# The first block of x in a slot of its own, 64 bytes out of step with the other fifteen

## The chip, the cores and the metric

The kernel runs on one core of one Trainium2 chip. The metric is the device time of one execution in microseconds, as the median of several runs. A profile of one execution stands beside the runs.

## The reference, cut to what matters

A decoder trunk of two layers on x of 256 tokens by 2048 features: an RWKV-7 time mix, a gated feed-forward layer with a causal convolution, a gated DeltaNet, and a second feed-forward layer, each followed by a layer norm of `ALPHA * x + f(x)`. Nearly all of the arithmetic is the product of x, or of a mixture of x with its shifted self, with large weight matrices:

```
r = xr @ w_r ; k = xk @ w_k ; v = xv @ w_v         # 2048 x 2048 each
proj = x @ w_in                                    # DeltaNet: 2048 x 12352
h = causal_dwconv(x @ w_up, conv_w) + conv_b       # feed-forward, twice: 2048 x 11008
gate, up = jnp.split(h, 2, axis=-1)
return (jax.nn.silu(gate) * up) @ w_down
```

## The kernel before, in words

**Blocks of x.** The 2048 features of an x are 16 blocks of 128. A block is one tile of 128 partitions by 512 float32r values: 256 tokens of the high part, then 256 of the low part (`split_act`, L677, makes the two: a rounded copy, and the rest). A product of two numbers so split takes three matmuls: high by high, high by low, low by high.

**Projections.** `proj_fm` (L687) makes up to 256 output features of a projection. Four times it loads 512 rows of weights into a tile `raw`, which ScalarE rounds into `whi` and VectorE (or GpSimd) turns into `wlo` (`weights`). Per block k of x and half b of the output there are three matmuls, with 128 columns of `whi` or `wlo` as the stationary operand and 256 columns of the block as the moving one; in the profile they are `mm<-xhl,whi` and `mm<-xhl,wlo`, or `mm<-mixhl,..` in the RWKV stage. They go k = 0 to 15 in order, 96 to a projection of 256 outputs, and every block is read again by every projection. For k = 0 the order of the three is high, high, low; for all others low, high, high:

```
for kk in range(4):
    for b in range(nb):
        for lo in (False, True) if i + kk == 0 else (True, False):
            product(tiles[i], i, kk, b, lo, ts)
```

The k projections (8) read an x that lies in slots of the RWKV stage's own pool (`slot`, L1063). The v projections (8) and r projections (8) read blocks that `mix` (L1066) takes from the pool `keep`. The up-projections of a feed-forward layer (`ffn`, L1507) are 22 for the gate and 22 for the up half, the last of each half as wide; DeltaNet (`gdn`, L1538) has 48 and a narrow one for its gates. Their x (`xhl`) is made by `ln_part` (L867): blocks 0 to 7 in `keep`, 8 to 15 in a pool of the stage (`hp`).

**The pool `keep`** has one kind of slot, `hl`, 2048 bytes per partition, 16 of them (`kept`, L670). At first they hold the 16 blocks of xv and then of xr; from the output projection of the RWKV stage on, 8 of them hold the residual `res` (L1211) to the end, and 8 the first half of x. In DeltaNet's output projection, the even ones of the 32 blocks `ohl` (L1640) take slots of `keep` too, the odd ones those of the stage. The last part of that projection keeps the blocks of seven weight tiles, 14 blocks, until the second half of the tokens is done.

**Addresses.** In the program as allocated, all weight tiles (`whi`, `wlo`, 4096 bytes each) begin at 0 modulo 128 bytes within a partition, every slice of them that a matmul loads too, and all blocks of x, in whichever pool, at 64 modulo 128. The tiles of a DeltaNet unit (`KQhi`, `KQlo`, both operands of the matmuls `kk`, and `S0hi`, `S0lo`) begin at 96.

**What sets the order.** A planner writes out the order of every engine's instructions beforehand (`Plan.order`): it goes by estimated costs, by which buffers of a pool are free, and fills TensorE's waits in the RWKV and DeltaNet units with projection matmuls. The up-projections have no such units beside them: there TensorE runs projection matmuls alone. SyncE issues all loads of weights.

The functions that the diff touches, and what calls them:

Of the kernel before, what the change touches and what calls it, by code (L numbers as in the profile page):

```python
# [13 lines left out]
F32R = mybir.dt.float32r  # L14
# [5 lines left out]
P = 128  # L20
T = 256
D = 2048
KB = D // P
# [596 lines left out]
class Trunk:  # L620
# [48 lines left out]

    def kept(self, dt, name):  # L670

        return self.keep.tile([P, 512], dt, tag="hl", bufs=KB, name=name)

    def hl(self, name, kept=False):
        return self.kept(F32R, name) if kept else self.hp.tile([P, 512], F32R, tag="hl", bufs=self.nhl, name=name)
# [191 lines left out]
    def ln_part(self, tb, chs):  # L867

        nc = self.nc
        gname, bname, li = self.ln  # L870
        for ch in chs:
            self.ln_norm(tb, ch)
            ps = self.sd("lnT")
            for j in range(4):
                kb = ch * 4 + j
                if tb == 0:
                    self.xk.append(self.hl("xhl", kb < KB // 2))
                self.tr(ps[:, j * P:(j + 1) * P], self.res[tb][ch][:, j * P:(j + 1) * P])
            for j in range(4):
                kb = ch * 4 + j  # L880
                t = self.tp.tile([P, P], F32, tag="lnt", bufs=NLNT, name="lnt")
                x, g, b = ps[:, j * P:(j + 1) * P], self.par(gname, li * KB + kb), self.par(bname, li * KB + kb)
                nc.either(("vector", "tensor_scalar", (t, x, g, b, ALU.mult, ALU.add), {}),
                          ("scalar", "activation", (t, x, AF.Identity), dict(scale=g, bias=b)))
                hi, lo = (self.xk[kb][:, o + tb * P:o + (tb + 1) * P] for o in (0, T))
                nc.copy(hi, t)
                nc.two(lo, t, hi.bitcast(F32), ALU.subtract)
# [178 lines left out]
    def mix(self, m, xk, ks=range(KB)):  # L1066

        for k in ks:
            x = self.slot([P, 512], F32R) if m == 2 else self.kept(F32R, "mixhl")
            t = self.xp.tile([P, T], F32, tag="mixt", bufs=3, name="mixt")  # L1070
            self.mixed(m, k, t)
            self.split_act(x[:, :T], x[:, T:], t)
            xk.append(x)
# [816 lines left out]
```

## Time and profile before

| | us |
|---|---|
| median of 3 runs (lowest, highest) | 3112.8 (3108.89, 3115.27) |
| the profiled execution | 3106.09 |
| its span, first to last instruction | 3104.4 |
| TensorE busy | 2996.5 (97% of the span) |
| its weight loads busy | 2801.8 (90%) |
| VectorE busy | 2163.8 (70%) |
| ScalarE busy | 1584.3 (51%) |
| GpSimd busy | 669.8 (22%) |

In order of time, the span holds the k, v and r projections with the RWKV units and the output projection (to about 695 us), the first feed-forward layer (up to 1190, down to 1430 us), DeltaNet (to about 2165 us) and its output projection (to 2370 us), and the second feed-forward layer. A busy TensorE isn't TensorE at its best: matmuls overlap in the records (one of 256 columns is recorded with 276 to 281 ns, though the next begins after some 113 to 118 ns), so how fast they follow each other is read by counting them in a stretch, or from their start times.

### The profile page before, as it was taken

What the parts mean: (1) busy time and instruction counts of PE and PEld (TensorE: products, weight loads), DVE (VectorE), ACT (ScalarE), POOL (GpSimd) and SP (SyncE); (2) the same over time, 40 slices, a digit from 0 to 9 for tenths busy, and PEclk for the clock granted to TensorE, in tenths of its full rate; (3) what the DMA queues carried; (4) which work ended last, traced back from release to release, by engine and by line L of the source; (5) the groups of instructions that cost most, each with busy time, mean ns of one, the idle gap of its engine ahead of it and who ended that gap; (6) DMA issues with size and microseconds to landing.
All of it is one profiled execution on the core that took longest, in us unless ns stands there. A gap on an engine that the chain in (4) does not pass through costs nothing.

```text
span 3104.4 us, 56128 instructions
## 1 busy us (share of the span) xinstructions
PE 2996.5 (97%) x22371; PEld 2801.8 (90%) x22371; DVE 2163.8 (70%) x3421; ACT 1584.3 (51%) x2584; POOL 669.8 (22%) x576
## 2 busy tenths in 40 slices
PE   8999999999999999998999999999999999999998
PEld 7998898779999998887999999998788999999886
DVE  7657878867666665447888888888677666666445
ACT  4436666445555554335455555555466555555333
POOL 3014334425101010003221121113143410101001
PEclk9998999999999999999999999999999999999999
DMA  6652222236666665655555555554455666666655
GB/s 198 207 165 87 67 65 89 71 119 202 189 186 188 185 188 183 194 192 161 171 148 146 144 148 147 153 144 129 149 189 181 203 185 189 184 189 185 192 190 186
DMA packets 436262, 503.77 MB, mean 162 GB/s; under 512 B 22784, under 2 KB 367264, under 8 KB 436000
## 3 DMA queue, kind: packets, MB, share of 16 engines
q1 hardware_dynamic: 436000, 500.19, 53.8%
q8 instruction: 175, 2.87, 0.4%
q14 instruction: 87, 0.71, 0.1%
HBM read 498.00 MB, written 2.13 MB: 161 GB/s over the span
## 4 chain that ended last, share of the span: by engine, by line
PE 82%; DVE 10%; POOL 3%; issue 2%; ACT 2%; DMA 1%; SPq 0%; DVEq 0%; POOLq 0%; ACTq 0%
PE mm L558 51%; PE tm L558 22%; DVE wlo L558 3%; PE y L558 1%; ACT whi L558 1%; PE au L558 1%; DVE uc L558 1%; PE n L558 1%; PE gm L558 1%; PE kv L558 1%; POOL lt L558 1%; POOL xhl L558 0%; PE o L558 0%; PE yT L558 0%; PE u L558 0%
## 5 line engine op out<-in xcount | busy, mean ns | idle before, releaser
L558 DVE TENSOR_TENSOR wlo<-raw,whi 128x1024 fp32r<-128x1024 f32 (+1 forms) x898 | 1113.5, 1241 | 629.6 <-ACT whi L558 626.9
L558 PE MATMUL mm<-xhl,whi 128*128 128x256 f32 x8584 | 1532.3, 283 | 5.1 <-DVE xhl L558 2.7
L558 ACT CAST whi<-raw 128x1024 fp32r<-128x1024 f32 (+2 forms) x917 | 939.5, 1026 | 854.4 <-PE mm L558 508.0
L558 PEld LDWEIGHTS mm<-xhl,whi 128*128 128x128 f32 x8584 | 1318.8, 190 | 8.2 <-POOL xhl L558 3.3
L558 PE MATMUL mm<-xhl,wlo 128*128 128x256 f32 (+1 forms) x4376 | 1212.1, 282 | 3.9 <-DVE wlo L558 3.1
L558 PEld LDWEIGHTS mm<-xhl,wlo 128*128 128x128 f32 x4376 | 819.4, 189 | 5.1 <-DVE wlo L558 3.4
L558 PE MATMUL tm<-whi,hhl 128*128 128x512 f32 x1312 | 406.6, 390 | 0.0
L558 DVE SCALAR_TENSOR_TENSOR acc<-mm,taps,acc 128x255 f32<-128x255 f32 (+1 forms) x522 | 248.3, 479 | 77.1 <-ACT acc L558 69.4
L558 PEld LDWEIGHTS tm<-whi,hhl 128*128 128x128 f32 x1312 | 246.3, 188 | 56.2
L558 PE MATMUL mm<-mixhl,whi 128*128 128x256 f32 x1536 | 281.6, 285 | 12.7 <-ACT mixhl L558 8.2
L558 POOL TENSOR_TENSOR hhl<-acc,hhl 128x256 fp32r<-128x256 f32 x84 | 101.4, 1208 | 755.9 <-ACT hhl L558 755.9
L558 PE MATMUL tm<-wlo,hhl 128*128 128x512 f32 x656 | 258.5, 394 | 0.8 <-DVE wlo L558 0.8
L558 PEld LDWEIGHTS mm<-mixhl,whi 128*128 128x128 f32 x1536 | 240.8, 195 | 16.1 <-ACT mixhl L558 8.2
L558 PE MATMUL mm<-mixhl,wlo 128*128 128x256 f32 x768 | 221.3, 293 | 4.7 <-DVE wlo L558 3.8
L558 ACT ACTIVATE acc<-mm,taps 128x256 f32<-128x256 f32 x230 | 124.1, 540 | 150.5 <-PE mm L558 150.3
L558 PE MATMUL tm<-whi,ohl 128*128 128x512 f32 x480 | 156.7, 399 | 0.1
L558 PEld LDWEIGHTS mm<-mixhl,wlo 128*128 128x128 f32 x768 | 147.4, 194 | 8.6 <-DVE wlo L558 4.8
L558 PEld LDWEIGHTS tm<-wlo,hhl 128*128 128x128 f32 x656 | 123.3, 188 | 25.6 <-DVE wlo L558 1.1
L558 POOL TENSOR_TENSOR wlo<-raw,whi 128x1024 fp32r<-128x1024 f32 (+2 forms) x19 | 44.0, 2315 | 444.9 <-ACT whi L558 440.8
L558 PEld LDWEIGHTS tm<-whi,ohl 128*128 128x128 f32 x480 | 90.7, 189 | 19.7 <-DVE z_u L558 0.7
L558 PE MATMUL tm<-wlo,ohl 128*128 128x512 f32 x240 | 94.0, 392 | 1.3 <-DVE wlo L558 1.3
L558 PE MATMUL tm<-whi,yhl 128*128 128x512 f32 x224 | 86.8, 427 | 1.4 <-ACT r_u L558 0.8
(342 smaller groups left out, 3349.6 us busy)
## 6 DMA issues: line engine op xcount, KB each, us to landing
raw<-in_ffn_w_up SPq DMA_DIRECT2D x336, 512.0 KB, 3.8
raw<-in_gdn_w_in SPq DMA_DIRECT2D x192, 512.0 KB, 3.8
raw<-in_ffn_w_down SPq DMA_DIRECT2D x168, 512.0 KB, 4.2
raw<-in_gdn_w_out SPq DMA_DIRECT2D x64, 512.0 KB, 3.8
raw<-in_rw_w_v SPq DMA_DIRECT2D x32, 512.0 KB, 4.3
raw<-in_rw_w_r SPq DMA_DIRECT2D x32, 512.0 KB, 3.6
raw<-in_rw_w_o SPq DMA_DIRECT2D x32, 512.0 KB, 3.7
raw<-in_rw_w_k SPq DMA_DIRECT2D x31, 512.0 KB, 4.5
```

Source lines behind the costliest of these rows:

```text
L558: i = getattr(getattr(self.real, o.eng), fn)(*(val(a) for a in args), **{k: val(a) for k, a in kw.items()})
```

## The change

Block 0 of every x that lies in `keep` gets a slot of its own, `x0`, of 544 values (2176 bytes per partition), and lies 16 values, 64 bytes, behind its beginning. The slots of the other kind become 15 instead of 16. `mix` and `ln_part` take block 0 there and the other blocks from the 15. `res` and `ohl` have only the 15 to choose from. The k projections' x and blocks 8 to 15 of `xhl` stay as they are. 2176 bytes are a multiple of 128, so that whatever lies behind keeps its place modulo 128; block 0 then begins at 0 modulo 128, where all the others begin at 64.

```
     def kept(self, dt, name):
 
-        return self.keep.tile([P, 512], dt, tag="hl", bufs=KB, name=name)
+        return self.keep.tile([P, 512], dt, tag="hl", bufs=KB - 1, name=name)
+
+    def block(self, k, name):
+
+        return self.kept(F32R, name) if k else self.keep.tile([P, 544], F32R, tag="x0", name=name)[:, 16:528]
...
                 if tb == 0:
-                    self.xk.append(self.hl("xhl", kb < KB // 2))
+                    self.xk.append(self.block(kb, "xhl") if kb < KB // 2 else self.hl("xhl"))
...
         for k in ks:
-            x = self.slot([P, 512], F32R) if m == 2 else self.kept(F32R, "mixhl")
+            x = self.slot([P, 512], F32R) if m == 2 else self.block(k, "mixhl")
```

## Rows read from the trace of the kernel before

**Rows 1.** The page, busy time of TensorE, and its granted clock in 40 slices.

```profile
PE 2996.5 (97%) x22371; PEld 2801.8 (90%) x22371; DVE 2163.8 (70%) x3421; ACT 1584.3 (51%) x2584; POOL 669.8 (22%) x576
...
PEclk9998999999999999999999999999999999999999
```

**Rows 2.** The page, the chain that ended last, by engine and by line.

```profile
PE 82%; DVE 10%; POOL 3%; issue 2%; ACT 2%; DMA 1%; SPq 0%; DVEq 0%; POOLq 0%; ACTq 0%
PE mm L558 51%; PE tm L558 22%; DVE wlo L558 3%; PE y L558 1%; ACT whi L558 1%; PE au L558 1%; DVE uc L558 1%; PE n L558 1%; PE gm L558 1%; PE kv L558 1%; POOL lt L558 1%; POOL xhl L558 0%; PE o L558 0%; PE yT L558 0%; PE u L558 0%
```

**Rows 3.** Stretches: busy us and instructions by engine, granted clock, DMA share, GB/s.

```profile
60.00:160.00 100.00, 100.00 (x884) 100.00 (x884) 63.02 (x87) 43.67 (x51) 2.94 (x2) 1.00 0.65 202
...
800.00:900.00 100.00, 100.00 (x851) 100.00 (x851) 62.25 (x80) 51.98 (x72) 9.72 (x8) 1.00 0.64 186
2500.00:2600.00 100.00, 100.00 (x851) 100.00 (x850) 62.08 (x80) 51.97 (x71) 10.93 (x9) 1.00 0.64 185
```

**Rows 4.** Groups by form, TensorE, in 60 to 160 and in 800 to 900 us.

```profile
L558 PE MATMUL mm<-mixhl,whi 128*128 128x256 f32 x590 | 99.8, 276 | 0.0
...
L558 PE MATMUL mm<-xhl,whi 128*128 128x256 f32 x568 | 99.7, 281 | 0.0
```

**Rows 5.** Timeline of TensorE (start, duration), in the v projection.

```profile
177.01 0.33 PE L558 MATMUL mm<-mixhl,wlo 128*128 128x256 f32 x1
177.18 0.40 PE L558 MATMUL mm<-mixhl,whi 128*128 128x256 f32 x2
```

**Rows 6.** Groups by form, TensorE, 178 to 196 us.

```profile
L558 PE MATMUL mm<-mixhl,whi 128*128 128x256 f32 x103 | 18.2, 281 | 0.0
L558 PE MATMUL mm<-mixhl,wlo 128*128 128x256 f32 x52 | 14.4, 281 | 0.0
```

**Rows 7.** Timeline of TensorE in the DeltaNet stage, behind `au` and behind `du`.

```profile
1656.82 0.83 PE L558 MATMUL au<-u,lt 128*128 128x128 f32 x6
...
1658.98 0.39 PE L558 MATMUL mm<-xhl,whi 128*128 128x256 f32 x2
...
1659.55 0.56 PE L558 MATMUL du<-rhr,y 128*128 128x128 f32 x4
...
1660.47 0.40 PE L558 MATMUL mm<-xhl,whi 128*128 128x256 f32 x2
```

**Rows 8.** Timeline: from the first and the last resumed stretch of that stage.

```profile
1512.68 0.39 PE L558 MATMUL mm<-xhl,whi 128*128 128x256 f32 x2
...
2158.16 0.39 PE L558 MATMUL mm<-xhl,whi 128*128 128x256 f32 x2
```

**Rows 9.** Timeline: `kk` without a wait: its first, and the next projection matmul.

```profile
1526.67 0.28 PE L558 MATMUL kk<-KQhi 128*128 128x256 f32 x1
...
1527.39 0.40 PE L558 MATMUL mm<-xhl,whi 128*128 128x256 f32 x2
...
1980.84 0.28 PE L558 MATMUL kk<-KQhi 128*128 128x256 f32 x1
...
1981.55 0.28 PE L558 MATMUL mm<-xhl,wlo 128*128 128x256 f32 x1
```

**Rows 10.** Stretches: both up-projections (TensorE alone); DeltaNet's output projection, all engines.

```profile
720.00:1180.00 460.00, 460.00 (x3909) 1.00 0.65 188
2380.00:2850.00 470.00, 470.00 (x3989) 1.00 0.65 188
...
2165.00:2370.00 205.00, 200.44 (x992) 164.74 (x991) 149.02 (x233) 113.12 (x197) 61.22 (x54) 0.99 0.52 169
```

**Rows 11.** Groups by form, TensorE, DeltaNet stage, 1440 to 2160 us.

```profile
L558 PE MATMUL mm<-xhl,whi 128*128 128x256 f32 x3020 | 542.3, 283 | 1.3 <-DVE xhl L558 1.3
L558 PE MATMUL mm<-xhl,wlo 128*128 128x256 f32 x1507 | 427.8, 288 | 0.0
```

**Rows 12.** Timeline: a `kk` that began after a wait, and the fast pace behind.

```profile
1612.25 0.28 PE L558 MATMUL kk<-KQhi 128*128 128x256 f32 x1
...
1613.72 0.39 PE L558 MATMUL mm<-xhl,whi 128*128 128x256 f32 x2
```

## The prediction

> **What bounds the kernel now.** I first read the page's busy shares: TensorE is busy for 97% of the span, with the granted clock at nine tenths or more in 39 of 40 slices and at eight in the other [rows 1]. The chain of waits agrees: 82% of the time to the last instruction lies on TensorE, 51% in the projections `mm`, whose moving operand is a block of x [rows 2]. So what matters is how fast consecutive projection matmuls follow each other, and that is read by counting them. In 100 us of the first projection (w_k) the engine starts 884 of them, one per 113.1 ns; in 100 us of either feed-forward up-projection it starts 851, one per 117.5 ns [rows 3]. Clock (1.00), shape and busy share (100.00 of 100 us) are the same, and the instruction itself lasts 276 ns in the one and 281 ns in the other [rows 3, 4]. There are thus two paces, **fast** and **slow**, 4.4 ns apart, with no idle time in either.
>
> The pace sticks. In the v projection a single late matmul (0.17 us to the next instead of 0.11) at 177.01 us ends the fast pace, and the 155 matmuls of the stretch 178 to 196 us all last 281 ns [rows 5, 6]. The up-projections run without a break and are slow from end to end. In the DeltaNet stage, where other small matmuls keep breaking in, the pace is drawn anew at each resumption: after `au` the projection runs fast, after `du`, 2.5 us later in the same projection, slow (where the timeline merges two matmuls, the pair takes 0.39 us at the fast pace and 0.40 us at the slow) [rows 7]. Over that stage I followed every resumption of 16 or more projection matmuls behind another tile: 66 stretches, 39 of them fast and 27 slow after the first few (the first and the last, both fast, are shown) [rows 8]. By count of matmuls the stage is about half and half.
>
> So the pace is not fixed by where x and the weights lie: the same addresses run at both. It is a phase between the matmul's stream and the weight load that runs beside it all the time (TensorE and its loader are both busy for 100.00 of 100 us [rows 3]). What starts a new phase can end the slow pace.
>
> **The change part by part.** *Block 0 moves by 64 bytes modulo 128.* In the program before, weight tiles begin at 0 and all blocks of x at 64 modulo 128; block 0 would now begin at 0, like the weights. It is read by the first 6 matmuls of each projection's 96, in 8 v, 8 r, 88 up and 49 DeltaNet projections, 153 in all (a few are narrower and have 3); the k projections keep their own slots. Nearest to such a matmul are the six `kk` matmuls of a DeltaNet unit: 256 columns too, in the same order of high and low parts, with both operands at 96 modulo 128. Their six take 0.72 us from 1526.67 us and 0.71 us from 1980.84 us, 118 to 120 ns each [rows 9]. Directly, block 0 costs between -4.4 and +2.5 ns a matmul against the slow pace: x 6 x 153 = -4.0 to +2.3 us. I take +1 us, near `kk`.
>
> *What the six do to the pace behind them* is the term that counts. No row shows this very disturbance, so I bound it. At best every slow stretch turns fast. The two uninterrupted up-projection stretches hold 3909 and 3989 matmuls in 460 and 470 us [rows 10]; at 113.1 ns the 7898 would take 893 us, 37 us less. The DeltaNet stage has 3020 + 1507 projection matmuls [rows 11], half slow: 2264 x 4.4 ns = 10 us. The v stretch gives 155 x 4.4 ns = 0.7 us, r, which is broken up throughout, I take at as much again. Together -48 us. At worst each disturbance leaves the slow pace behind it: the up-projections stay as they are, the fast half of the DeltaNet stage is lost (10 us), and so are the fast parts of v and r, about 1 us: +11 us.
>
> I take a value on the fast side, because that is where most new phases ended: 39 of 66, and of the twelve `kk` groups of the stage that began after a wait nine were followed by the fast pace, the one shown after four matmuls [rows 12]. In the up-projections nothing else breaks in, so whatever pace block 0 leaves holds to the next block 0. I charge 10 of 96 matmuls a projection (the six and four to settle): 86/96 of 37 us is 33 us. In the DeltaNet stage the units still redraw the pace in between, so only half of the 10 us comes: 5 us. With 1 us of v and r and the direct +1 us the sum is **-38 us**.
>
> Is TensorE still the bound then? At the fast pace the up-projection's weights must come at 186 x 884/851 = 193 GB/s; the w_k stretch takes 202 GB/s with TensorE still at 100.00 of 100 us. VectorE (62.25 of 100 us) and ScalarE (51.98) would rise by the same 4% to some 65 and 54 [rows 3]. So the cover holds and nothing else becomes late.
>
> A rule stands against all this. In the trace, loads and matmuls run side by side at two paces [rows 3]. The Trainium skill, TensorE: Matmul & The Clock Gate, section "Step-by-step: what each phase is for", says the opposite of contention: "Loading the next tile's weights doesn't steal SBUF read bandwidth from the running matmul." By that rule the address of x can't matter and the sum would be 0; the two paces at one clock and one shape speak against it, but none of them shows that an address matters.
>
> *The slot of its own and the 15 other slots.* 128 bytes more per partition, and no instruction, DMA or wait added. After the r projections the residual takes 8 of the 15 slots; 7 and the new one are the 8 that the first half of x needs. `res[0]` now takes the slot of block 1 instead of block 0, freed six matmuls, 0.7 us, later; the output projection's work covers it. In DeltaNet's output projection the kept blocks `ohl` have 7 slots instead of 8, and the last stage of it holds just 7 until its second half. TensorE is busy there for 200.44 of 205 us [rows 10]; if a block came late, the wait would be part of the idle 4.6 us or at most about as much again. The planner writes a slightly different order; I cost it at nothing, with about 3 us either way, the size of the spread of the runs. Edits to `mix` and `ln_part` only choose the slot.
>
> **The sum** is made against the profiled execution: 3106.1 us, of which 3104.4 us are span; less 38 gives 3068. It lies 6.7 us under the median of the runs shown, 3112.8 us, so the forecast for the median is 3112.8 - 38 = 3075 us. About 6 us (0.2%) is what a measurement of this kernel can tell from no change.
>
> **The rivals.**
> *The slow pace is what block 0 leaves.* This is the one that ends slower. For it: three times `kk` came in without any wait, as block 0 does, once in a fast stretch (at 1526.67 us) and twice in slow ones (one shown, at 1980.84 us), and the projection behind was slow each time [rows 9]. Against it: there the loads before and behind the six differ by 32 bytes from their partners, which those of block 0 don't. It decides if the matmuls of block 1 start slow in an up-projection: +11 us and +1 us for the six, 3124 us. Chance 0.27.
> *Nothing moves.* Either the address doesn't matter (the rule above), or six matmuls are too few and each pace survives them: within 3 us of 3113. For it: no row shows a change of pace by address alone; against it, the single late matmul at 177.01 us was enough [rows 5]. Chance 0.20.
> *The two paces alternate*, or only one of the two entries into the feed-forward stages is caught: half of 38, about 3094 us. Chance 0.08.
>
> **How the numbers follow.** The forecast, slow to fast and then fast to fast, has 0.45; its own range is 3065 us (all 48 us) to 3085 us (28 us, with longer settling). Faster by over 0.2%: 0.45 + 0.08 = 0.53; within: 0.20; slower: 0.27. As cases of both signs hold the most, the range must reach from the forecast's best, 3062 us with the spread of the runs, to the slow rival with its spread, 3126 us.
>
> **What would show it.** Right: in the up-projections 100 us hold about 880 matmuls instead of 851, the form `mm<-xhl,whi` has a mean near 276 ns instead of 281, its slow matmuls stand in the first ten of each 96, and DMA there rises towards 193 GB/s. The stretch from 178 us on is fast again from its next projection. Wrong: 851 again with 281 ns in the up-projections; then either the DeltaNet stage keeps its mixture (nothing moves) or its fast stretches end at the next block 0 (the slow rival). New idle time of TensorE behind `ohl` would show that the missing slot was felt.

## The result, and the profile after

| | before | after |
|---|---|---|
| median of 5 runs, us | 3109.3 (3103.2 to 3115.3) | 3127.4 (3121.7 to 3141.5) |
| ratio, with its 95% interval | | 1.0069 (1.0044 to 1.0094) |
| the profiled execution, us | 3106.1 | 3127.4 |
| its span, us | 3104.4 | 3125.7 |
| TensorE busy, us | 2996.5 | 3026.9 |

The change makes the kernel slower by 0.7%, where 1.2% faster was forecast. The first view to read is again the one by stretches; its columns are those of [rows 3], for TensorE alone. This is the changed kernel: k projections, first up-projection, first down-projection, DeltaNet, second up-projection.

```profile
60.00:160.00 100.00, 100.00 (x850) 1.00 0.65 197
800.00:900.00 100.00, 100.00 (x850) 1.00 0.65 188
1260.00:1360.00 100.00, 100.00 (x430) 1.00 0.60 191
1440.00:2160.00 720.00, 684.95 (x5842) 0.98 0.53 148
2500.00:2600.00 100.00, 100.00 (x850) 1.00 0.65 186
```

The same view of the kernel before, for the two stretches that [rows 3] doesn't have:

```profile
1260.00:1360.00 100.00, 100.00 (x439) 1.00 0.60 190
1440.00:2160.00 720.00, 682.12 (x5907) 0.98 0.53 150
```

Three things are to be seen. The up-projections have 850 matmuls in 100 us instead of 851: the change as a whole moved their pace by next to nothing. The k projections fell from 884 to 850, though their x holds no block out of step and they run before any such block is read. And the 512-column matmuls of the down-projection, which don't read x at all (their stationary operand is a block of `hhl`, the hidden activations, and the weights are the moving one), went from 439 to 430 in 100 us (227.8 to 232.6 ns each). Times per matmul here are 100 us over the count; a count takes in those still running when the stretch begins, so from start to start they are 0.2 to 1 ns longer. A slowdown ahead of block 0, and one in matmuls that never touch it, can't come from block 0.

DeltaNet's stage shows the same. Behind `au`, where the projection ran fast before [rows 7], the timeline of the changed kernel has it slow (pairs of 0.40 us):

```profile
1666.46 1.05 PE L558 MATMUL au<-u,lt 128*128 128x128 f32 x8
...
1667.47 0.40 PE L558 MATMUL mm<-xhl,whi 128*128 128x256 f32 x2
...
1668.88 0.40 PE L558 MATMUL mm<-xhl,whi 128*128 128x256 f32 x2
```

Counted as for [rows 8], 64 of 65 resumed stretches are slow now, 1 fast. The groups by form, for 60 to 160 and for 800 to 900 us, tell one thing more (compare [rows 4]): the mean of the slow matmul is 279 to 280 ns here, neither the old fast 276 nor the old slow 281, in both stretches alike.

```profile
L558 PE MATMUL mm<-mixhl,whi 128*128 128x256 f32 x567 | 99.7, 279 | 0.0
L558 PE MATMUL mm<-mixhl,wlo 128*128 128x256 f32 x283 | 77.7, 280 | 0.0
...
L558 PE MATMUL mm<-xhl,whi 128*128 128x256 f32 x567 | 99.8, 279 | 0.0
L558 PE MATMUL mm<-xhl,wlo 128*128 128x256 f32 x283 | 78.0, 280 | 0.0
```

Where the 21 us lie is read from the start times in the timelines, from the first matmul of each stage to that of the next, in the last row to its last matmul (us, one profiled execution each; the last column is the wide slot of the second experiment below):

| stage | before | after | wide slot |
|---|---|---|---|
| k and v projections, from the span's start | 196.8 | 202.5 | 196.2 |
| r, RWKV units, output projection | 499.1 | 498.3 | 494.8 |
| up, first | 493.5 | 493.9 | 477.4 |
| down, first | 239.0 | 242.7 | 239.1 |
| DeltaNet | 733.9 | 739.0 | 738.7 |
| its output projection | 201.0 | 202.7 | 201.2 |
| up, second | 492.8 | 493.7 | 477.9 |
| down, second | 236.0 | 240.8 | 237.0 |

Of the 21.5 us between before and after, 5.7 lie in k and v, 8.5 in the two down-projections, 5.1 in DeltaNet (where one kernel's length differs by 3 us from execution to execution, see below), 1.7 in its output projection, and 1.3 in the up-projections, which were forecast to carry nearly the whole effect (the r stage took 0.8 less).

### The profile page after: what moved, and what is told of

It reads as the page before. It is cut to its first block, busy times and chain, and to the rows that moved or that the text cites. A ratio compares the mean times of both kernels' runs of the same rounds, so it can differ in the third digit from the quotient of the medians.

```text
span 3125.7 us, 56127 instructions
## 1 busy us (share of the span) xinstructions
PE 3026.9 (97%) x22371; PEld 2821.5 (90%) x22371; DVE 2166.7 (69%) x3422; ACT 1585.9 (51%) x2585; POOL 670.2 (21%) x574
## 4 chain that ended last, share of the span: by engine, by line
PE 83%; DVE 10%; POOL 3%; issue 2%; ACT 2%; DMA 1%; SPq 0%; DVEq 0%; POOLq 0%; ACTq 0%
PE mm L558 51%; PE tm L558 22%; DVE wlo L558 2%; PE y L558 1%; ACT whi L558 1%; DVE uc L558 1%; PE au L558 1%; PE n L558 1%; PE gm L558 1%; PE kv L558 1%; POOL lt L558 0%; DVE acc L558 0%; PE o L558 0%; PE du L558 0%; PE u L558 0%
## 5 line engine op out<-in xcount | busy, mean ns | idle before, releaser
L558 PE MATMUL tm<-whi,hhl 128*128 128x512 f32 x1312 | 413.4, 395 | 0.0
L558 PEld LDWEIGHTS tm<-whi,ohl 128*128 128x128 f32 x480 | 90.6, 189 | 21.5 <-DVE z_u L558 0.7
```

The costliest lines, as they stand in the source:

```text
L558: i = getattr(getattr(self.real, o.eng), fn)(*(val(a) for a in args), **{k: val(a) for k, a in kw.items()})
```

## The experiments

Theory A is that the 128 bytes which the new slot adds, and by which it pushes everything behind it away from the weight tiles, set the pace. Theory B is that block 0 out of step leaves the slow pace behind it (the slow rival of the prediction). Theory C is that the missing slot and the altered order of the work cost the time. The distance of a block is its address less that of the weight tiles, modulo 256, from the programs as allocated: 192 for all blocks before; after the change 64 for all but block 0, and 0 for block 0. The blocks of `hhl` lie at the same distance from the weights as those of x, but in their matmuls the two roles are swapped.

**1. The push alone** (`e1_pad128`). A tile of the small pool ahead of `keep` gets 128 unused bytes:

```
-        self.stats = [self.tp.tile([P, 4, 6], F32, name=f"stats{tb}") for tb in range(2)]
+        self.stats = [self.tp.tile([P, 24 + 32], F32, name="stats0")[:, :24].rearrange("p (c s) -> p c s", c=4),
+                      self.tp.tile([P, 4, 6], F32, name="stats1")]
```

> The kernel before with 128 unused bytes per partition ahead of the pool keep: all sixteen blocks of x, and every pool behind, lie 128 bytes further, no block is out of step, and there are 16 slots again. Theory A (the 128 bytes by which the new slot pushes everything behind it away from the weights set the pace): slow as the changed kernel or a few us less, 3118 to 3128 us; 850 matmuls in 60 to 160 us of the k projections instead of 884, tm<-whi,hhl 233 ns apart instead of 229. Theory B (block 0 out of step leaves the slow pace behind it): as before, 3103 to 3115 us, 884 and 229. Theory C (15 slots and another order of the work): as before.

Measured: 3123.8 us against 3106.0, ratio 1.0059 (1.0044 to 1.0075). The stretches:

```profile
60.00:160.00 100.00, 100.00 (x852) 1.00 0.63 196
800.00:900.00 100.00, 100.00 (x851) 1.00 0.65 189
1260.00:1360.00 100.00, 100.00 (x430) 1.00 0.59 188
```

The 852 and 430 of the changed kernel are there without its block 0, its slot or its order. Theory A holds; B and C are not needed for most of the loss.

**2. The same change without the push** (`e2_wide_slot`). The slot becomes 128 bytes wider, so that all behind it moves by 256 bytes and is at distance 192 again; block 0 stays 64 bytes out of step.

```
-        ... self.keep.tile([P, 544], F32R, tag="x0", name=name)[:, 16:528]
+        ... self.keep.tile([P, 576], F32R, tag="x0", name=name)[:, 16:528]
```

> The changed kernel with a slot of 576 values instead of 544 for block 0: block 0 is 64 bytes out of step as in the change, and there are 15 other slots, but all that lies behind has moved by 256 bytes instead of 128. Theory A, if what counts is the place modulo 256: near the kernel before, 3105 to 3117 us, with 884 matmuls in 60 to 160 us and 229 ns for tm, and only block 0's own cost of some 2 us. Theory A, if any move counts: slow, 3118 to 3130 us. Theory B: slow in the up-projections and in DeltaNet, 3118 to 3130 us, with the k projections at 884. Theory C: slow as well.

Measured: 3076.5 us against 3106.0, ratio 0.9919 (0.9888 to 0.9950). None of the expectations had that:

```profile
60.00:160.00 100.00, 100.00 (x883) 1.00 0.66 201
800.00:900.00 100.00, 100.00 (x882) 1.00 0.65 191
1260.00:1360.00 100.00, 100.00 (x439) 1.00 0.60 192
1440.00:2160.00 720.00, 682.29 (x5873) 0.98 0.53 149
2500.00:2600.00 100.00, 100.00 (x882) 1.00 0.66 192
```

The up-projections are fast, 882 instead of 851, and the down-projection is back at 439. So the distance counts modulo 256, not by any move, and theory B falls the other way round: at distance 192 block 0 leaves the *fast* pace behind it. The timeline shows it at work at the beginning of a projection (block 0's first matmul is the third of the four that the first row merges):

```profile
807.61 0.62 PE L558 MATMUL mm<-xhl,whi 128*128 128x256 f32 x4
808.07 0.28 PE L558 MATMUL mm<-xhl,wlo 128*128 128x256 f32 x1
808.18 0.40 PE L558 MATMUL mm<-xhl,whi 128*128 128x256 f32 x2
808.42 0.40 PE L558 MATMUL mm<-xhl,wlo 128*128 128x256 f32 x2
808.65 0.40 PE L558 MATMUL mm<-xhl,whi 128*128 128x256 f32 x2
808.89 0.28 PE L558 MATMUL mm<-xhl,wlo 128*128 128x256 f32 x1
809.01 0.39 PE L558 MATMUL mm<-xhl,whi 128*128 128x256 f32 x2
809.24 0.28 PE L558 MATMUL mm<-xhl,wlo 128*128 128x256 f32 x1
809.35 0.39 PE L558 MATMUL mm<-xhl,whi 128*128 128x256 f32 x2
```

Some ten matmuls run unevenly, then the pairs take 0.39 us to the end of the projection. In the changed kernel the same place ends in the slow pace (0.40 us):

```profile
809.33 0.65 PE L558 MATMUL mm<-xhl,whi 128*128 128x256 f32 x4
809.81 0.29 PE L558 MATMUL mm<-xhl,wlo 128*128 128x256 f32 x1
809.94 0.40 PE L558 MATMUL mm<-xhl,whi 128*128 128x256 f32 x2
...
811.12 0.40 PE L558 MATMUL mm<-xhl,whi 128*128 128x256 f32 x2
```

**3. Block 0 in its slot, but in step** (`e3_flat_slot`): `[:, 16:528]` of the change becomes `[:, :512]`.

> The changed kernel with block 0 at the beginning of its own slot of 544 values: it is no longer 64 bytes out of step modulo 128; the slot still pushes all behind it by 128 bytes. Theory A: as slow as the changed kernel, 3120 to 3130 us, 850 matmuls in 60 to 160 us. Theory B: as before, 3103 to 3115 us, 884. Theory C: slow, but with the k projections at 884.

Measured: 3121.6 us, ratio 1.0054 (1.0038 to 1.0071); 852 and 852 matmuls, and 430. As theory A expects: where all else is at distance 64, block 0's step makes no difference that can be measured (the interval of the changed kernel holds this ratio). Block 0 isn't quite level here: at 192 modulo 256 it differs from the other blocks by 128 bytes, which mattered as little.

**4. Another distance** (`e4_pad64`): the first experiment's edit with 64 bytes.

> The kernel before with 64 unused bytes ahead of the pool keep: all blocks of x lie 64 bytes further, so that they and the weight tiles begin at the same place modulo 128. Theory A: the pace changes everywhere, k projections and tm included; to which side is open, 3065 to 3135 us. Theories B and C: as before, 3103 to 3115 us, as no block is out of step and no slot is missing.

Measured: 3129.5 us, ratio 1.0074 (1.0056 to 1.0093). The projections are slower than any seen before, 836 and 835 in 100 us (119.7 ns), and the 512-column matmuls faster, 443 instead of 439. The two kinds of matmul don't want the same distance.

**5. The wide slot with block 0 in step** (`e5_wide_flat`), the control of the second experiment: `[:, :512]` of 576.

> The wide slot of the second experiment (576 values, all behind it 256 bytes further) with block 0 at its beginning, so that no block is out of step modulo 256: it differs from that experiment by the 64 bytes of block 0 alone. If block 0 out of step is what turned the up-projections fast there: slow up-projections again (851 matmuls in 800 to 900 us, 117.8 ns apart), k projections fast (884), and 3100 to 3113 us, like the kernel before. If the 256 bytes or the 15 slots did it: 3073 to 3080 us with 880 matmuls.

Measured: 3108.7 us over 10 runs, ratio 1.0020 (0.9992 to 1.0047); 851 in the up-projections.

```profile
60.00:160.00 100.00, 100.00 (x851) 1.00 0.64 196
800.00:900.00 100.00, 100.00 (x851) 1.00 0.65 187
1260.00:1360.00 100.00, 100.00 (x438) 1.00 0.61 193
```

So the 64 bytes of block 0 alone are worth the 30 us of the second experiment, and the 15 slots and the new order cost nothing that can be measured: theory C falls. One expectation missed: the k projections were slow in this execution, where they were fast in others at the same distance (before, and in experiments 2, 10 and 12). At 192 one stage can thus have either pace in different executions; that a single program changes it from one execution to the next is not shown, since none was traced with both.

**6 to 8. More distances**, one execution each: 192, 224 and 32 bytes in the place of 64.

> The kernel before with 192 unused bytes ahead of the pool keep: x at 0 modulo 256, weights at 128. If the place modulo 256 sets the pace, it differs from the 64-byte run (120.0 ns for every projection matmul, 226.5 for tm), although both have x and weights level modulo 128. If only modulo 128 counts there: the same 120.0 and 226.5 ns, 3125 to 3135 us.

> The kernel before with 224 unused bytes ahead of the pool keep: x 32 bytes short of its old place modulo 256. If the pace hangs on the place modulo 256, one pace for each stage that is neither the old 113.3 and 117.8 ns nor need it lie between them; 3060 to 3150 us. If only multiples of 64 bytes count: as before.

> The kernel before with 32 unused bytes ahead of the pool keep: x 32 bytes past its old place. If the pace hangs on the place modulo 256: another pace than with 224 bytes, 3060 to 3150 us. If only multiples of 64 bytes count: as before, 3101 to 3115 us, with 884 matmuls in 60 to 160 us.

Measured, with the runs above, as matmuls in 100 us (k projections; first up-projection; 512-column ones of the first down-projection):

| distance | run | 60 to 160 us | 800 to 900 us | 1260 to 1360 us | median, us |
|---|---|---|---|---|---|
| 192 | before | 884 | 851 | 439 | 3106.0 to 3109.6 |
| 224 | 32 bytes | 847 | 847 | 430 | 3125.2 (1 run) |
| 0 | 64 bytes | 836 | 835 | 443 | 3129.5 |
| 64 | 128 bytes | 852 | 851 | 430 | 3123.8 |
| 128 | 192 bytes | 845 | 835 | 430 | 3137.2 (1 run) |
| 160 | 224 bytes | 845 | 855 | 430 | 3119.9 (1 run) |
| 192 | wide slot in step | 851 | 851 | 438 | 3108.7 |

0 and 128 bytes, level modulo 128 both, differ (443 against 430): the place modulo 128 isn't enough, and the place modulo 256 repeats. Steps of 32 bytes count too. Of the distances tried, only 192 shows the pace of 884 (32 and 96 weren't tried). But 192 isn't alone in having two paces. At 128 the two up-projections, whose blocks lie at the same distance, differ within one execution:

```profile
800.00:900.00 100.00, 100.00 (x835) 1.00 0.63 182
2500.00:2600.00 100.00, 100.00 (x845) 1.00 0.65 187
```

At 160 the k projections have 845 and the up-projections 855.

**9. Weights and x pushed together** (`e9_pad_all128`): 128 bytes ahead of the weight tiles.

```
-        self.mhalf = self.cp.tile([P, 16], F32, name="mhalf")
+        self.mhalf = self.cp.tile([P, 48], F32, name="mhalf")[:, :16]
```

> The kernel before with 128 unused bytes ahead of the weight tiles: weights and x both lie 128 bytes further, and keep their distance modulo 256. If the distance of x from the weights counts: as before, 3100 to 3113 us, with fast and slow stretches side by side in DeltaNet (some 40 of 66 resumed stretches fast) and tm near 229 ns. If the place of x by itself counts: slow as in the first experiment, 3118 to 3127 us, hardly a fast stretch, tm at 233 ns.

Measured: 3106.8 us over 10 runs, ratio 0.9999 (0.9976 to 1.0022); 439 in 1260 to 1360 us, and of the resumed stretches of DeltaNet's stage 41 of 67 fast. The distance between the two operands counts, not where x lies by itself. The k projections had the slow pace again (852). The pushes also move tiles that the other engines touch, but the pace doesn't follow those engines: in 800 to 900 us, by the start times, matmuls beside a busy VectorE and matmuls beside an idle one both follow each other after 117.8 ns (the kernel before and the first experiment) or 120.0 ns (the fourth).

**10 and 11. The wide slot again, and with the k projections out of step too.** The eleventh gives their block 0 a slot of 576 values as well:

```
-            x = self.slot([P, 512], F32R) if m == 2 else self.block(k, "mixhl")
+            x = self.block(k, "mixhl") if m != 2 else (self.slot([P, 512], F32R) if k else
+                    self.xp.tile([P, 576], F32R, tag="m0", name="mixhl")[:, 16:528])
...
-NMIX = 23
+NMIX = 22
```

> The kernel of the second experiment once more, for its time beside the next one: 3073 to 3080 us again if block 0 out of step pulls every execution to the fast pace; spread up to 3105 us, as in the kernel before, if the run of the second experiment drew the fast pace by chance.

> The second experiment with block 0 of the k projections' x out of step as well (a slot of 576 values in their own pool, 22 other slots there instead of 23). If block 0 out of step pulls the pace to fast wherever x and weights lie 192 modulo 256 apart: the k projections are fast in every execution (about 880 matmuls in 60 to 160 us), which takes up to 5 us off the executions that drew the slow pace there and costs 0.4 us in the others: 3070 to 3077 us. Rival, the k projections keep the pace that they begin with: as the second experiment.

Measured beside each other: 3076.0 us, ratio 0.9896 (0.9871 to 0.9921), and 3074.7 us, ratio 0.9894 (0.9868 to 0.9920). The gain of the second experiment is no chance. The step in the k projections stays unsettled: both profiled executions had them fast (883 and 882), and the times don't tell the two apart.

**12. The change word for word, with the push completed to 256 bytes from outside** (`e12_after_pad128`): the edit of the first experiment, in the changed kernel. Block 0 lies 64 bytes short of the others modulo 256 (distance 128) instead of 64 past.

> The changed kernel word for word (slot of 544 values) with 128 unused bytes ahead of the pool keep: all but block 0 lie 256 bytes further than before the change, as in the second experiment, and block 0 lies 64 bytes short of them modulo 256 instead of 64 bytes past. If only the 128 bytes behind the slot spoilt the change: fast, with 880 matmuls in 800 to 900 us and 3070 to 3095 us, whichever way block 0 is out of step. If it has to be 64 bytes past: slow up-projections, 851, 3100 to 3120 us.

Measured: 3076.8 us against 3109.6, ratio 0.9907 (0.9875 to 0.9939):

```profile
60.00:160.00 100.00, 100.00 (x883) 1.00 0.65 202
800.00:900.00 100.00, 100.00 (x881) 1.00 0.67 195
2500.00:2600.00 100.00, 100.00 (x881) 1.00 0.66 193
```

128 unused bytes elsewhere turn the changed kernel's loss of 0.7% into a gain of 0.9%. And the step works with block 0 at distance 0 or 128; other steps weren't tried. Over all traces with the rest of x at 192, the eight up-projections with block 0 out of step (experiments 2, 10, 11, 12) have 881 or 882 matmuls in 100 us, and the six without (before, experiments 5 and 9) 851 or 852.

## Why the prediction was wrong

*What bounds the kernel* held: the time follows the pace of the matmuls, and the two paces and their sticking were read rightly from [rows 3, 5, 7].

*The step that failed* is the one about the slot of its own: "128 bytes more per partition, and no instruction, DMA or wait added", costed at nothing but an altered order. What made it look free was that 2176 is a multiple of 128. The runs show that the distance between moving and stationary operand counts modulo 256. So the slot took every block behind it, in all pools, from distance 192, where a fast pace exists, to 64, where none was seen in a long stretch. That alone is the first experiment's +18 us, 1.0059. The reading "the pace is not fixed by where x and the weights lie" was true at 192, where I had looked, and was carried too far: both paces at one distance show that the distance isn't all, not that it is nothing.

*Block 0's effect* was forecast rightly for a layout in which the other blocks stay at 192, as the prediction had in mind. That it ends on the fast side was partly luck: the side was taken from a count of other interruptions (39 of 66) and given 0.45, and why the six matmuls leave the fast pace behind them stays open. In the second experiment the two up-projections take 16.1 and 14.9 us less, 31 us against the 33 of the sum, and the kernel 29.5 us less than the one before measured beside it, against 38. After the push there is no fast pace to fall into, and the six matmuls are left with their direct price: 850 matmuls in 100 us against 851 in the first experiment's up-projection is one matmul, 0.12 us, in nearly nine projections, or 13 ns each; times 153 that is about 2 us, near the +1 of the sum. As it rests on a difference of one in a count, this is no more than an estimate; the two up-projections are 1.3 us longer than in the first experiment (493.9 and 493.7 us against 493.5 and 492.8).

*The DeltaNet term* failed by itself: 5 us of gain were charged. The wide slot's DeltaNet stage takes 738.7 us against 733.9, with TensorE starting 5873 matmuls in 1440 to 2160 us against 5907; the same kernel again took 735.5 us, and the eleventh and twelfth experiments 733.8 and 738.6. No gain shows in any of the four. In the other direction the term overshot as well: losing the fast half was to cost 10 us, and nearly every stretch slow cost 5.1 us (1.8 in the first experiment, 735.7). Two executions of one kernel differ by 3.2 us here, so not even these are surely the pace's. The pace there doesn't carry through to the stage's length; what takes its place I didn't isolate.

*The slow rival* had the sign and some 60% of the size (+12 us against +18 to +21), by the wrong mechanism: block 0 doesn't leave the slow pace behind. Its sum was also cut short: 3112.8 + 12 us and 3 us of spread are 3128 us, where the range ended at 3126; had it held the measured 3127, that would have been luck. The three `kk` groups that spoke for it [rows 9] came in and went out with other distances than block 0, as the text said against it. *The rule* of the Trainium skill (TensorE: Matmul & The Clock Gate, "Step-by-step: what each phase is for"), by which a weight load takes no read bandwidth from a running matmul, was taken to make the sum 0. That conclusion doesn't agree with the runs: 128 bytes of distance, with no other edit, moved the kernel by 0.59%. Whether it is read bandwidth that the load takes, no run here shows.

*The other covers* held: the residual's later slot and the 7 slots of `ohl` show no new wait (in DeltaNet's output projection TensorE is idle for 3.5 of 202.7 us, before for 4.6 of 201.0), and at the fast pace the weights came in time, at 191 to 195 GB/s with TensorE at 100.00 of 100 us, as [rows 3] had let expect.

## What to carry to other kernels

An edit that moves tiles, even one that only makes a pool larger, changes the distance between the two operands of every matmul that has one of them ahead of the edit and one behind it; compare the addresses of the two programs, and count matmuls per 100 us in stretches that the edit doesn't touch, before explaining anything by the edit itself. When a stream of equal matmuls shows two paces, try the addresses modulo 256 in steps of 32 bytes, each with one unused tile, and keep the distance at which the fast pace exists, if the other matmuls (here those of 512 columns) don't lose more by it. Where both paces live at one distance, try one block out of step at the head of each pass: at 192 it put the stream on the fast pace for the price of ten uneven matmuls, at 64 it did nothing that could be measured.

## What the runs showed of the hardware

The time from one 256-column matmul to the next (weights loaded for each) was 113.1 ns, or 117.0 to 119.7, at one clock, by the distance of the two operands' addresses modulo 256 and by the phase that the stream happened to be in (two paces at 192, 128 and 160); the 512-column ones took from 225.7 to 232.6 ns. From start to start these are 113.3, 117.3 to 120.0, and 226.7 to 233.3 ns. The phase outlives hundreds of matmuls, and one late matmul, or at 192 six at another distance, ended it. Single executions of the kernel before ranged from 3083 to 3129 us; how much of that is the phase isn't shown, as the longest also had the lowest mean granted clock (0.980, the others 0.982 to 0.992), and the shortest were not traced. What in the memory or the array makes the period 256 bytes, no run here shows.
